# A pair of experts' scatter in the middle of the next odd expert, in float32r with bare one-hots

## The chip, the cores and the metric

One Trainium2 chip, one of its cores. The metric is device time in microseconds (us) of one execution. The engines are named as in the profile: PE is TensorE's matmul (PEld its weight load), DVE is VectorE, ACT is ScalarE, POOL is GpSimd, SP is SyncE, which issues the DMAs.

## The reference, cut to what matters

256 tokens of width 1024 pass a mixing layer (an SSD group beside an MLA group), and then a mixture of experts, in which each token goes to 4 of 32 experts:

```python
def moe_ffn(h, w_router, b_router, w_gate_up, b_gate_up, w_down, b_down):
    logits = (h @ w_router).astype(jnp.float32) + b_router.astype(jnp.float32)
    top_vals, top_idx = lax.top_k(logits, TOP_K)
    gates = jax.nn.softmax(top_vals, axis=-1)
    ...
    def expert_block(args):
        tok, g, e = args
        xb = h[tok]
        gu = xb @ w_gate_up[e] + b_gate_up[e]
        glu = jnp.minimum(gu[:, :D_FF_EXPERT], SWIGLU_LIMIT)
        lin = jnp.clip(gu[:, D_FF_EXPERT:], -SWIGLU_LIMIT, SWIGLU_LIMIT)
        act = glu * jax.nn.sigmoid(SWIGLU_ALPHA * glu) * (lin + 1.0)
        y = act @ w_down[e] + b_down[e]
        return y * g[:, None].astype(y.dtype)
    ...
    return jax.ops.segment_sum(y.reshape(n_slots, d), slot_tok, num_segments=n_tok)
```

All weights are float32: 8 MB of w_gate_up and 4 MB of w_down for each expert, 384 MB in all.

## The kernel before, in words

The mixing layer and the router take the first 185 us. Then a loop runs over the experts e = 0 to 31 (`last` is 31). For each expert there are four weight tiles of 2 MB for the way up (gu{e}_0 to gu{e}_3) and two for the way down (dn{e}_0, dn{e}_1). They come through one DMA queue of SP, in a fixed order (L230), into nine slots of 2 MB; a transfer starts when the matmuls that read its slot's last content have ended. Four experts (0, 2, 3, 31) give their first tile free early ("ahead"); the others give all four up tiles free at the end of the way up.

An expert has room for 64 tokens (CAP). Its tokens are gathered by a matmul with one-hot columns (`gather`, oh on DVE, pg on PE L1231, copied to xg), transposed (`gathered`, pgt L1239) and modulated on DVE in two steps (xT, L1241 and L1242). `up` (L1252) multiplies by the weights, tile for tile; `act` copies the sums (gs), transposes them (tp, L1272), adds the bias on DVE (u), and makes the minimum, the sigmoid (ACT) and two products (sg, ac; L1284 to L1288). `down` (L1300) multiplies ac by the down tiles into one PSUM buffer (py), and `keep_down` copies it into half of each of two tiles (cm0, cm1), so that two experts, an even one and the odd one before or after it, fill them together. `scatter` (L1332 to L1339) adds such a pair's rows to the tokens' sums: four sums of 128x512 (pc, two PSUM buffers), each one matmul of the gated one-hots (gtm) by cm, added to acc by DVE. In f32 one such matmul shows as two instructions in the trace. The gated one-hots are made by `spread_cols` (go, eight instructions on DVE) and `spread_mats` (four transposes L1324, an ACT copy L1326). PSUM: one buffer (tag "sm") serves pg and both pgt, one serves py, tp and pc have two.

PE's order is the program's; DVE's and ACT's is made by a scheduler. In iteration e PE does: the first up tile; gather of e+1; down of e-1 (`finish_down`); the second up tile; the transposes of xT for e+1; the other two up tiles; the transposes of act(e). For even e the scatter of the pair (e-2, e-1) stands between the way up and act(e) (for e = 30 it is the pair (28,29), behind act(30)), and four transposes for the pair's one-hots follow act. Tokens beyond 64 of an expert are handled in a branch (`overflow`), which stands behind up, for the four experts "ahead" behind the first up tile; whether it is taken is known only on the chip, and all engines read the count at that place (releaser names with a q, as DVEq L1417, are waits for an engine to come to such a branch). In the loop's last two iterations the order differs: down(29) is ahead of up(30), down(30) ahead of up(31), and the last pair (30, 31) is scattered after the loop.

The lines of before that matter most:

```python
        gs = up_out(gu, "g1b", A.copy if e == last else V.tensor_copy)
        if not ahead:
            overflow(e, wg, wd, f"pr{(e + ahead) % 2}")
        ...
        pair = e > 0 and e % 2 == 0
        if pair and e < last - 1:
            scatter(lambda t, ch: gt[:, ch, t, :], lambda ch: comb[ch], bias)
        ...
        ac = act(e, gs, 2 if e == last else 1)
        if pair and e == last - 1:
            scatter(lambda t, ch: gt[:, ch, t, :], lambda ch: comb[ch])
```

## Time and profile before

| | |
|---|---|
| median of 3 runs | 1159.1 us (1157.83 to 1161.47) |
| the profiled execution's own time | 1159.5 us |
| its span | 1157.7 us, granted clock 0.977 on the mean |
| PE busy | 1069.6 us (92%) |
| DVE, ACT, POOL busy | 419.8, 191.1, 69.5 us |
| DMA | 449.21 MB, 388 GB/s on the mean |

The span is from the first instruction to the last; the time has 1.8 us more around it. Busy shares are means over stages with different limits, so they don't tell which engine a microsecond on the path belongs to. The granted clock is TensorE's, as a share of full speed. A row of the timeline gives start, duration, engine, line, what is written from what, how many instructions are merged, and in brackets the idle time of that engine before them with what ended it.

### The profile page before, as it was taken

The page shows a single profiled execution, that of the slowest core. Times are in us where ns is not written, and L with a number is a line of the kernel's source. Part 1 is how long each engine was busy: PE and PEld are TensorE (multiplying, and loading weights), DVE is VectorE, ACT ScalarE, POOL GpSimd, SP SyncE. Part 2 cuts the span into 40 slices and gives each one's busy share as a digit, 9 for nine tenths or more (in the row PEclk, how much of TensorE's full clock was granted, in tenths as well). Part 3 has the DMA queues.
Part 4 walks back from the last instruction along what each step waited for, and adds up shares of the span by engine and source line. Part 5 has one row for each costly group of instructions (what it writes and reads, how often), then busy time and mean ns, then how long its engine had stood idle before and what let it go on. Part 6 is the DMA issues. An engine that isn't in the chain of part 4 may idle for free. (4 is left out here: it accounts for less than half of the span.)

```text
span 1157.7 us, 13070 instructions
## 1 busy us (share of the span) xinstructions
PE 1069.6 (92%) x5125; PEld 456.0 (39%) x5128; DVE 419.8 (36%) x892; ACT 191.1 (17%) x366; POOL 69.5 (6%) x68
## 2 busy tenths in 40 slices
PE   5999998989999999899989998999899998999996
PEld 3886674333333333333323332333323332333333
DVE  3358755333333323232322333142313232323224
ACT  5464433110111111001000101010101010101003
POOL 0274330000000000000000000000000000000000
PEclk9999999999999999899989999999989998999998
DMA  9959679968989999999999999999999999999982
GB/s 341 354 227 368 243 280 417 380 266 354 412 351 427 427 427 429 426 428 427 427 427 428 428 427 427 428 428 425 430 427 428 426 429 428 420 421 428 428 357 74
DMA packets 47713, 449.21 MB, mean 388 GB/s; under 512 B 6741, under 2 KB 11062, under 8 KB 21210
## 3 DMA queue, kind: packets, MB, share of 16 engines
q1 hardware_dynamic: 47162, 447.41, 93.0%
q8 instruction: 75, 1.23, 0.4%
q14 instruction: 60, 0.49, 0.1%
q10 hardware_dynamic: 416, 0.07, 0.0%
HBM read 446.42 MB, written 1.05 MB: 387 GB/s over the span
## 5 line engine op out<-in xcount | busy, mean ns | idle before, releaser
L1252 PE MATMUL gu<-gu,xT 128*64 128x512 f32 x2048 | 474.8, 612 | 30.5 <-DMA gu<-in_w_gate_up 28.5
L1252 PEld LDWEIGHTS gu<-gu,xT 128*64 128x64 f32 x2048 | 146.5, 140 | 308.9 <-issue 272.4
L1300 PE MATMUL py<-dn,ac 128*64 128x512 f32 x992 | 218.9, 594 | 0.2 <-DVE ac L1288 0.2
L1300 PEld LDWEIGHTS py<-dn,ac 128*64 128x64 f32 x992 | 70.7, 137 | 143.0 <-issue 133.6
L1309 DVE COPY cm<-py 64x512 f32<-64x512 f32 x30 | 20.8, 694 | 210.9 <-ACT cm L1308 210.9
L1258 DVE COPY gs<-gu 128x512 f32<-128x512 f32 x31 | 21.4, 692 | 174.9 <-PE gu L1252 174.9
L1257 ACT COPY gs<-gu 128x512 f32<-128x512 f32 x32 | 18.8, 586 | 317.5 <-PE gu L1252 317.5
L1338 PE MATMUL pc<-cm,gtm 128*128 128x512 f32 x120 | 59.3, 620 | 11.7 <-DVEq L1417 10.3
L1231 PE MATMUL pg<-x,oh 128*64 128x512 f32 x256 | 60.6, 594 | 3.6 <-DVEq L1417 1.9
L1339 DVE TENSOR_TENSOR acc<-acc,pc 128x512 f32<-128x512 f32 x64 | 44.0, 688 | 38.2 <-PE pc L1338 38.1
L1596 POOL TENSOR_TENSOR x<-x,acc 128x512 f32<-128x512 f32 x1 | 1.3, 1263 | 917.8 <-ACT acc L1595 917.8
L1241 DVE TENSOR_TENSOR xT<-pgt,md 128x512 f32<-128x512 f32 x32 | 22.1, 692 | 86.4 <-PE pgt L1239 86.4
L1279 DVE TENSOR_TENSOR u<-tp,biasT 128x512 f32<-128x512 f32 x64 | 41.5, 685 | 29.5 <-PE tp L1272 29.3
L1308 ACT COPY cm<-py 64x512 f32<-64x512 f32 x30 | 17.4, 579 | 189.6 <-PE py L1300 189.6
L1272 PEld LDWEIGHTS tp<-ident,gs 128*128 128x128 f32 x256 | 34.8, 208 | 27.8 <-ACTq L1417 16.4
L1227 DVE TENSOR_SCALAR oh<-cst,rkp,r 128x64 f32<-128x64 f32 x64 | 17.2, 311 | 76.8 <-PE pg L1231 76.8
L1272 PE MATMUL tp<-ident,gs 128*128 128x128 f32 x256 | 38.2, 290 | 6.5 <-PEq L1417 5.3
L1338 PEld LDWEIGHTS pc<-cm,gtm 128*128 128x128 f32 x120 | 19.3, 188 | 51.3 <-DVEq L1417 20.0
L1233 ACT COPY xg<-pg 128x512 f32<-128x512 f32 x32 | 18.7, 586 | 121.8 <-PE pg L1231 121.7
L1285 ACT ACTIVATE sg<-u 128x512 f32<-128x512 f32 (+1 forms) x33 | 20.4, 618 | 95.3 <-DVE u L1284 91.8
L1231 PEld LDWEIGHTS pg<-x,oh 128*64 128x64 f32 x256 | 18.1, 137 | 40.9 <-issue 39.9
L1316 DVE TENSOR_SCALAR go<-cst,rkp,gate 128x64 f32<-128x64 f32 x128 | 30.0, 308 | 0.6 <-DVEq L1417 0.6
(432 smaller groups left out, 943.3 us busy)
## 6 DMA issues: line engine op xcount, KB each, us to landing
gu<-in_w_gate_up SPq DMA_DIRECT2D x128, 2048.0 KB, 21.4
dn<-in_w_down SPq DMA_DIRECT2D x62, 2048.0 KB, 29.1
w2w<-in_w_ada SPq DMA_DIRECT2D x6, 1024.0 KB
w0w<-in_w_ada SPq DMA_DIRECT2D x5, 1024.0 KB, 6.9
w0w<-in_w_ada SPq DMA_DIRECT2D x6, 512.0 KB, 6.5
w2w<-in_w_ada SPq DMA_DIRECT2D x6, 512.0 KB
w4w<-in_w_ada SPq DMA_DIRECT2D x3, 1024.0 KB, 8.7
w4w<-in_w_out SPq DMA_DIRECT2D x3, 1024.0 KB
```

Source lines behind the costliest of these rows:

```text
L1231: T.matmul(pg[64 * h : 64 * h + 64, :], oh[:, t, :], x[:, t, h * 512 : h * 512 + 512], start=t == 0, stop=t == TT - 1)
L1241: V.tensor_tensor(xT.rearrange("p (h q) s -> p q h s", h=2), pg, a2.rearrange("p (h q) -> p q h", h=2)[:, :, :, None].to_broadcast([P, 4, ...
L1252: T.matmul(gu[h][64 * g : 64 * g + 64, :], xT[:, k, :], ws(k)[:, g * 1024 + h * 512 : g * 1024 + h * 512 + 512], start=k == 0, stop=k == K ...
L1258: copy(gs[1], gu[1])
L1272: T.transpose(tp[f // 4][:, f % 4].rearrange("p g s -> p (g s)"), gs[f // 4][:, rows_of(f % 4)], ident)
L1279: V.tensor_tensor(u[:, hs], tp[h], bv[:, hs, :, None].to_broadcast([P, 4, 2, CAP]), op=OP.add)
L1285: A.activation(sg[:, fs], u[:, fs, 0, :], AF.Sigmoid, scale=1.702)
L1300: T.matmul(py[64 * g : 64 * g + 64, :], ac[:, f, :], wd(f, ch), start=f == 0, stop=f == FT - 1)
L1309: V.tensor_copy(comb[(e & 1) ^ 1][64:128, :], py[64:128, :])
L1316: V.tensor_scalar(go[:, t, j, :], iota, rkp[:, t, ee : ee + 1], gate[:, t, ee : ee + 1], op0=OP.is_equal, op1=OP.mult)
L1338: T.matmul(pc, lhs(t, ch), rhs(ch), start=bias is None or (t, ch) != bias_left[0], stop=True)
L1339: V.tensor_tensor(acc[:, t, ch * 512 : ch * 512 + 512], acc[:, t, ch * 512 : ch * 512 + 512], pc, op=OP.add)
```

## The change

The scatter of a pair moves. In an even expert it no longer stands between up and act; the pair (e-2, e-1) is scattered in the next iteration, e+1, behind down(e) and ahead of the second up tile. For e = 30 the pair (28, 29) is scattered between the second and the third up tile. The operands change: the one-hots are bare (is_gt on DVE, from PSUM, in place of the ACT copy), the gate of each row is the sum of its gated one-hots (a reduction on DVE), and `gated` (in place of the copies) multiplies the down result by it into two float32r tiles, hi and lo, of which ACT makes hi and DVE lo; each sum of a scatter has then two float32r matmuls. The overflow's scatter changes in the same way. The last pair stays in f32 with gated one-hots. The one-hots for a gather (`slots`) are formed an expert earlier.

```diff
@@ -1220,11 +1220,14 @@
     acc = tl([P, TT, D], "acc", "f1")
     iota = cst[:, CIO : CIO + CAP]
-    def gather(e):
-
+    def slots(e):
         oh = tl([P, TT, CAP], "oh", f"oh{e % 2}")
         for t in range(TT):
             V.tensor_scalar(oh[:, t, :], iota, rkp[:, t, e : e + 1], r2[:, t : t + 1], op0=OP.is_equal, op1=OP.mult)
+        return oh
+
+    def gather(oh):
+
         pg = mp.tile([P, 512], F32, tag="sm", name="pg")
         for t in range(TT):
             for h in range(2):
@@ -1301,12 +1304,18 @@
                          start=f == 0, stop=f == FT - 1)
         return py
+    def gated(hi, lo, src, by):
+
+        A.activation(hi, src, AF.Copy, scale=by)
+        V.scalar_tensor_tensor(lo, src, by, hi, op0=OP.mult, op1=OP.subtract)
+
     def keep_down(e, py):
         if e % 2 == 0:
-            comb[0] = tl([P, 512], "cm0", "pv2")
-            comb[1] = tl([P, 512], "cm1", "bn")
-        A.copy(comb[e & 1][0:64, :], py[0:64, :])
-        V.tensor_copy(comb[(e & 1) ^ 1][64:128, :], py[64:128, :])
+            for ch in range(2):
+                comb[ch] = [tl([P, 512], f"c{j}{ch}", (("pv2", "cl0"), ("bn", "cl1"))[ch][j], F32R) for j in range(2)]
+        for g in range(2):
+            ch, r = (e & 1) ^ g, slice(64 * g, 64 * g + 64)
+            gated(comb[ch][0][r, :], comb[ch][1][r, :], py[r, :], gts[-1][1][r, ch : ch + 1])
     def spread_cols(es):
@@ -1316,15 +1325,23 @@
                 V.tensor_scalar(go[:, t, j, :], iota, rkp[:, t, ee : ee + 1], gate[:, t, ee : ee + 1], op0=OP.is_equal, op1=OP.mult)
         return go
-    def spread_mats(go, tag="bgr"):
+    turn = [0]
+
+    def spread_mats(go, bare=True):
         pg = mp.tile([P, 2, TT, P], F32, tag="sm", name="pgt")
         for ch in range(2):
             for t in range(TT):
                 T.transpose(pg[:, ch, t, :], go[:, t, 2 * ch : 2 * ch + 2, :].rearrange("p j s -> p (j s)"), ident)
-        gt = tl([P, 2, TT, P], "gtm", tag)
-        A.copy(gt, pg)
-        return gt
+        gt = tl([P, 2, TT, P], "gtm", ("bgr", "bgr1")[turn[0]] if bare else "cbs", F32R if bare else F32)
+        if not bare:
+            A.copy(gt, pg)
+            return gt
+        V.tensor_scalar(gt, pg, 0.0, None, op0=OP.is_gt)
+        by = tl([P, 2], f"by{turn[0]}")
+        turn[0] = 1 - turn[0]
+        V.tensor_reduce(by, pg.rearrange("p c t q -> p c (t q)"), axis=AX.X, op=OP.add)
+        return gt, by
     bias_left = [(t, ch) for t in range(TT) for ch in range(2)]
@@ -1335,7 +1352,9 @@
                 pc = mp.tile([P, 512], F32, tag=tag, name="pc", bufs=2)
                 if bias is not None and (t, ch) == bias_left[0]:
                     T.matmul(pc, bias[:, t, :], end[0:NE, D + ch * 512 : D + ch * 512 + 512], start=True, stop=False)
-                T.matmul(pc, lhs(t, ch), rhs(ch), start=bias is None or (t, ch) != bias_left[0], stop=True)
+                hi, lo = rhs(ch)
+                T.matmul(pc, lhs(t, ch), hi, start=bias is None or (t, ch) != bias_left[0], stop=False)
+                T.matmul(pc, lhs(t, ch), lo, start=False, stop=True)
                 V.tensor_tensor(acc[:, t, ch * 512 : ch * 512 + 512], acc[:, t, ch * 512 : ch * 512 + 512], pc, op=OP.add)
     def warm(n):
@@ -1376,7 +1396,8 @@
         for t in range(TT):
             for ch in range(2):
                 T.transpose(pg[:, t, ch, :], go[:, t, ch : ch + 4].rearrange("p j s -> p (j s)"), ident)
-        A.copy(ovt, pg)
+        V.tensor_scalar(ovt, pg, 0.0, None, op0=OP.is_gt)
+        V.tensor_reduce(by, pg.rearrange("p t c q -> p (t c q)"), axis=AX.X, op=OP.add)
         gu = mp.tile([P, 512], F32, tag="py", name="guo")
         for k in range(KT):
             for j in range(4):
@@ -1397,9 +1418,10 @@
         V.tensor_scalar(u[:, :, 1], u[:, :, 1], -7.0, 1.0, op0=OP.max, op1=OP.add)
         V.tensor_tensor(ovs, ovs, u[:, :, 0], op=OP.mult)
         V.tensor_tensor(ovs, ovs, u[:, :, 1], op=OP.mult)
-        return ovt
-
-    def ov_down(wd, ovt):
+        return ovt, by
+
+    def ov_down(wd, spread):
+        ovt, by = spread
         py = mp.tile([P, 512], F32, tag="py", name="pyo")
         for i in range(4):
             for z in range(2):
@@ -1407,8 +1429,8 @@
                 for ch in range(2):
                     o = 64 * z + 32 * ch
                     T.matmul(py[o : o + OV, :], ovs[:, f % 4, f // 4, :], wd(f, ch), start=i == 0, stop=i == 3)
-        yo = tl([P, 512], "yo", "md1")
-        A.copy(yo, py)
+        yo = [tl([P, 512], f"yo{j}", ("md1", "pt1")[j], F32R) for j in range(2)]
+        gated(*yo, py, by)
         scatter(lambda t, ch: ovt[:, t, ch, :], lambda ch: yo)
     def overflow(e, wg, wd, tag):
@@ -1450,8 +1472,10 @@
         return end[:, 0:D]
     G.memset(acc, 0.0)
-    gs = wd = gt = None
-    xT = gathered(0, gather(0))
+    gs = wd = gt = bias = None
+    gts = []
+    xT = gathered(0, gather(slots(0)))
+    oh = slots(1)
     e4 = tl([P, TT, 4], "e4")
     tc.keep_in_program_order(V.tensor_tensor(e4, m8[:, :, 0:4], m8[:, :, 0:1].to_broadcast([P, TT, 4]), op=OP.subtract))
     A.activation(e4, e4, AF.Exp)
@@ -1473,11 +1497,21 @@
         return lambda k: ts_[k // 2][:, k % 2 * 2 * FF : k % 2 * 2 * FF + 2 * FF]
     def finish_down(e, ac, wd):
-        keep_down(e, down(e, ac, wd, e & 1))
+
+        py = down(e, ac, wd, e & 1)
+        if e % 2 == 0 and e > 0:
+            scatter_pair(gts[-2])
+        keep_down(e, py)
         for j in range(2):
             st_.done(f"dn{e}_{j}")
-    bias = None
+    def scatter_pair(gt):
+        nonlocal bias
+        scatter(lambda t, ch: gt[0][:, ch, t, :], lambda ch: comb[ch], bias)
+        if bias is not None:
+            bias_left.pop(0)
+            bias = bias if bias_left else None
+
     last = ne - 1
     for e in range(ne):
         wg = weights_up(e)
@@ -1496,7 +1530,9 @@
             overflow(e, wg, wd, f"pr{(e + ahead) % 2}")
             st_.done(f"gu{e}_0")
         if e < last - 1:
-            xg = gather(e + 1)
+            xg = gather(oh)
+            if e < last - 2:
+                oh = slots(e + 2)
         if 0 < e < last - 1:
             finish_down(e - 1, ac, wdp)
         up(gu, xT, wg, range(2, 4))
@@ -1506,6 +1542,8 @@
             go = spread_cols((e, e + 1, e + 1, e))
         if e == 19:
             g2b = gain()
+        if e == last - 1:
+            scatter_pair(gts[-1])
         up(gu, xT, wg, range(4, 8))
         xT = xTn if e < last - 1 else xTl
         gs = up_out(gu, "g1b", A.copy if e == last else V.tensor_copy)
@@ -1516,23 +1554,15 @@
         if e == 9:
             end = late[0]
             bias = gates_by_expert()
-        pair = e > 0 and e % 2 == 0
-        if pair and e < last - 1:
-            scatter(lambda t, ch: gt[:, ch, t, :], lambda ch: comb[ch], bias)
-            if bias is not None:
-                bias_left.pop(0)
-                bias = bias if bias_left else None
         ac = act(e, gs, 2 if e == last else 1)
-        if pair and e == last - 1:
-            scatter(lambda t, ch: gt[:, ch, t, :], lambda ch: comb[ch])
-        if e == last - 1:
+        if e % 2 == 0 and e < last - 1:
+            gts.append(spread_mats(go))
+        elif e == last - 1:
             gt = gtl
-        elif e % 2 == 0:
-            gt = spread_mats(go)
         if e == last - 2:
-            xTl = gathered(last, gather(last))
-            gtl = spread_mats(spread_cols((last - 1, last - 1, last, last)), "cbs")
+            xTl = gathered(last, gather(slots(last)))
+            gtl = spread_mats(spread_cols((last - 1, last - 1, last, last)), False)
     tc.keep_in_program_order(A.activation(epsw, epsc, AF.Sqrt))
```

How the instructions stand at three places. The first is the end of expert 2 and the middle of expert 3. On PE from the end of up(2) to the first up tile of expert 3, before (gu_2 and gu_3 are expert 2's last two up tiles, pc<-cm the scatter of the pair (0,1)):

```order
L1252 MATMUL gu<-gu_2_2061,xT 64x512 x8
L1252 MATMUL gu<-gu_3_2429,xT 64x512 x8
L1338 MATMUL pc<-cm_2055,gtm 128x512
L1338 MATMUL pc<-cm_2056,gtm 128x512
L1338 MATMUL pc<-cm_2055,gtm 128x512
L1338 MATMUL pc<-cm_2056,gtm 128x512
L1272 MATMUL tp<-ident,gs_2733 128x128 x4
L1272 MATMUL tp<-ident,gs_2734 128x128 x4
L1324 MATMUL pgt<-ident,go 128x128 x4
L1252 MATMUL gu<-gu_0_2435,xT 64x512 x8
```

In the change:

```order
L1255 MATMUL gu<-gu_2_2078,xT 64x512 x8
L1255 MATMUL gu<-gu_3_2462,xT 64x512 x8
L1275 MATMUL tp<-ident,gs_2776 128x128 x4
L1275 MATMUL tp<-ident,gs_2777 128x128 x4
L1335 MATMUL pgt<-ident,go 128x128 x4
L1255 MATMUL gu<-gu_0_2468,xT 64x512 x8
```

The scatter's four matmuls are gone from here. They stand in expert 3 now, on PE between down(2) (py) and the second up tile (gu_1), with c as the gated down results in their two parts:

```order
L1234 MATMUL pg<-x,oh 64x512 x4
L1303 MATMUL py<-dn_0_2464,ac 64x512 x8
L1303 MATMUL py<-dn_1_2466,ac 64x512 x8
L1356 MATMUL pc<-c_2068,gtm 128x512
L1357 MATMUL pc<-c_2069,gtm 128x512
L1356 MATMUL pc<-c_2070,gtm 128x512
L1357 MATMUL pc<-c_2071,gtm 128x512
L1356 MATMUL pc<-c_2068,gtm 128x512
L1357 MATMUL pc<-c_2069,gtm 128x512
L1356 MATMUL pc<-c_2070,gtm 128x512
L1357 MATMUL pc<-c_2071,gtm 128x512
L1255 MATMUL gu<-gu_1_2698,xT 64x512 x8
```

Each of the four sums is two matmuls now, one for hi and one for lo, and the second up tile stands behind them. On DVE the same place, act(2), before (gs the copied sums, acc<-acc,pc the scatter's additions; the last two rows read the count for the overflow's branch):

```order
L1258 COPY gs_2734<-gu 128x512
L1339 TENSOR_TENSOR acc<-acc,pc 128x512 x4
L1279 TENSOR_TENSOR u<-tp,biasT 128x512 x2
L1316 TENSOR_SCALAR go<-cst,rkp,gate 128x64 x8
L1284 TENSOR_SCALAR u<-u 128x1024
L1286 TENSOR_SCALAR u<-u 128x8x64
L1287 TENSOR_TENSOR sg<-sg,u 128x512
L1288 TENSOR_TENSOR ac<-sg,u 128x512
L1416 TENSOR_LOAD cnt
L1417 COMPARE_AND_BRANCH
```

In the change:

```order
L1261 COPY gs_2777<-gu 128x512
L1282 TENSOR_TENSOR u<-tp,biasT 128x512 x2
L1340 TENSOR_SCALAR gtm<-pgt 128x512
L1343 TENSOR_REDUCE by_2813<-pgt 128x2
L1325 TENSOR_SCALAR go<-cst,rkp,gate 128x64 x3
L1287 TENSOR_SCALAR u<-u 128x1024
L1325 TENSOR_SCALAR go<-cst,rkp,gate 128x64 x5
L1289 TENSOR_SCALAR u<-u 128x8x64
L1290 TENSOR_TENSOR sg<-sg,u 128x512
L1291 TENSOR_TENSOR ac<-sg,u 128x512
L1438 TENSOR_LOAD cnt
```

The four additions are gone from here; is_gt (gtm) and the reduction (by) stand between u and the minimum, and five of the one-hots stand behind the minimum.

The second place is the start of the loop on DVE, before (xT are the two steps of expert 0's gathered rows; e, d, eq and gate are the softmax over the four chosen experts; the eight gated one-hots of the pair (0,1), go, follow behind the branch):

```order
L1227 TENSOR_SCALAR oh<-cst,rkp,r_1523 128x64 x4
L1241 TENSOR_TENSOR xT<-pgt,md_112 128x4x2x64
L1242 TENSOR_TENSOR xT<-xT,md_112 128x512
L1456 TENSOR_TENSOR e_1717<-m_1525 128x8
L1459 TENSOR_REDUCE d_1720<-e_1717 128x2
L1460 RECIPROCAL d_1720<-d_1720 128x2
L1461 TENSOR_TENSOR e_1717<-e_1717,d_1720 128x8
L1463 TENSOR_TENSOR eq<-eq,e_1717 128x128 x2
L1464 TENSOR_REDUCE gate<-eq 128x64
L1416 TENSOR_LOAD cnt
L1417 COMPARE_AND_BRANCH
```

In the change:

```order
L1226 TENSOR_SCALAR oh<-cst,rkp,r_1523 128x64 x2
L1480 TENSOR_TENSOR e_1720<-m_1525 128x8
L1483 TENSOR_REDUCE d_1723<-e_1720 128x2
L1484 RECIPROCAL d_1723<-d_1723 128x2
L1485 TENSOR_TENSOR e_1720<-e_1720,d_1723 128x8
L1226 TENSOR_SCALAR oh<-cst,rkp,r_1523 128x64 x2
L1487 TENSOR_TENSOR eq<-eq,e_1720 128x128 x2
L1488 TENSOR_REDUCE gate<-eq 128x64
L1244 TENSOR_TENSOR xT<-pgt,md_112 128x4x2x64
L1325 TENSOR_SCALAR go<-cst,rkp,gate 128x64 x5
L1245 TENSOR_TENSOR xT<-xT,md_112 128x512
L1325 TENSOR_SCALAR go<-cst,rkp,gate 128x64 x3
```

The softmax stands ahead of xT's first step now, and five of the eight one-hots stand between xT's two steps.

The third place is the end of expert 30 on PE, before (tp are act(30)'s transposes, pc the scatter of the pair (28,29), py is down(30), gu_0 expert 31's first up tile):

```order
L1272 MATMUL tp<-ident,gs_13277 128x128 x4
L1272 MATMUL tp<-ident,gs_13278 128x128 x4
L1338 MATMUL pc<-cm_12783,gtm 128x512
L1338 MATMUL pc<-cm_12784,gtm 128x512
L1338 MATMUL pc<-cm_12783,gtm 128x512
L1338 MATMUL pc<-cm_12784,gtm 128x512
L1300 MATMUL py<-dn_0_13159,ac 64x512 x8
L1300 MATMUL py<-dn_1_13161,ac 64x512 x8
L1252 MATMUL gu<-gu_0_13163,xT 64x512 x8
```

In the change:

```order
L1275 MATMUL tp<-ident,gs_13829 128x128 x4
L1275 MATMUL tp<-ident,gs_13830 128x128 x4
L1303 MATMUL py<-dn_0_13693,ac 64x512 x8
L1303 MATMUL py<-dn_1_13695,ac 64x512 x8
L1255 MATMUL gu<-gu_0_13697,xT 64x512 x8
```

Down(30) follows the transposes directly; the scatter of the pair stands within up(30).

## Rows read from the trace of the kernel before

**Rows 1.** The page's slices: PE's busy tenths, the DMA engines' share, GB/s.

```profile
PE   5999998989999999899989998999899998999996
...
DMA  9959679968989999999999999999999999999982
GB/s 341 354 227 368 243 280 417 380 266 354 412 351 427 427 427 429 426 428 427 427 427 428 428 427 427 428 428 425 430 427 428 426 429 428 420 421 428 428 357 74
```

**Rows 2.** The page's DMA issues: count, KB each, median us to landing.

```profile
gu<-in_w_gate_up SPq DMA_DIRECT2D x128, 2048.0 KB, 21.4
```

**Rows 3.** Timeline of PE, experts 6 to 9: start us, us, instructions, [idle before].

```profile
395.58 3.89 PE L1338 MATMUL pc<-cm,gtm 128*128 128x512 f32 x8 [1.03 <-DVEq L1417]
399.31 1.11 PE L1272 MATMUL tp<-ident,gs 128*128 128x128 f32 x8
...
400.79 3.65 PE L1252 MATMUL gu<-gu,xT 128*64 128x512 f32 x16
...
424.63 1.21 PE L1272 MATMUL tp<-ident,gs 128*128 128x128 f32 x8 [0.40 <-PEq L1417]
...
455.19 3.23 PE L1252 MATMUL gu<-gu,xT 128*64 128x512 f32 x14
```

**Rows 4.** The waits of PE by releaser: us in total, times, longest.

```profile
PE gu L1252 <- DMA gu<-in_w_gate_up: 28.5, 12, 5.3
```

**Rows 5.** Timeline of PE at weight waits of experts 10, 14 and 28.

```profile
483.07 5.39 PE L1252 MATMUL gu<-gu,xT 128*64 128x512 f32 x12 [1.98 <-DMA gu<-in_w_gate_up]
...
602.76 6.41 PE L1252 MATMUL gu<-gu,xT 128*64 128x512 f32 x16 [4.59 <-DMA gu<-in_w_gate_up]
...
1020.42 5.35 PE L1252 MATMUL gu<-gu,xT 128*64 128x512 f32 x16 [1.94 <-DMA gu<-in_w_gate_up]
```

**Rows 6.** Windows: busy us of each engine, granted clock, DMA share, GB/s.

```profile
335.00:340.00 5.00, 5.00 (x26) 1.71 (x24) 0.17 (x1) 0.04 (x1) 0.00 (x0) 1.00 0.55 231
340.00:345.00 5.00, 4.71 (x15) 1.73 (x12) 2.82 (x5) 0.55 (x1) 0.00 (x0) 1.00 0.66 208
...
600.00:612.00 12.00, 9.24 (x30) 2.84 (x32) 2.19 (x5) 1.14 (x2) 0.00 (x0) 0.72 1.01 429
```

**Rows 7.** Timeline of SP's queue: the issue that up(4) holds back.

```profile
340.86 0.33 SPq L230 DMA_DIRECT2D gu<-in_w_gate_up  x1
```

**Rows 8.** Timeline of PE, two float32r matmuls of L482 to L484.

```profile
170.22 0.39 PE L482 MATMUL pm<-whi,mix 128*128 128x512 f32 x1
170.45 0.39 PE L483 MATMUL pm<-whl,mix 128*128 128x512 f32 x1
```

**Rows 9.** Groups of DVE instructions: count | busy us, mean ns | idle before.

```profile
L1339 DVE TENSOR_TENSOR acc<-acc,pc 128x512 f32<-128x512 f32 x64 | 44.0, 688 | 38.2 <-PE pc L1338 38.1
...
L817 DVE TENSOR_REDUCE mx<-at 128x2 f32<-128x512 f32 x4 | 2.7, 687 | 0.4 <-PE at L815 0.4
```

**Rows 10.** Timeline of PE and of DVE, expert 0.

```profile
190.04 3.65 PE L1252 MATMUL gu<-gu,xT 128*64 128x512 f32 x16 [1.51 <-DVE xT L1242]
...
215.50 1.08 PE L1300 MATMUL py<-dn,ac 128*64 128x512 f32 x4 [0.21 <-DVE ac L1288]
...
192.45 1.88 DVE L1316 TENSOR_SCALAR go<-cst,rkp,gate 128x64 f32<-128x64 f32 x8 [0.56 <-DVEq L1417]
```

**Rows 11.** Timeline of PE, from the scatter behind up(2) to gather(4).

```profile
285.12 3.96 PE L1338 MATMUL pc<-cm,gtm 128*128 128x512 f32 x8
288.91 1.12 PE L1272 MATMUL tp<-ident,gs 128*128 128x128 f32 x8
...
295.97 1.94 PE L1231 MATMUL pg<-x,oh 128*64 128x512 f32 x8 [1.91 <-DVEq L1417]
```

**Rows 12.** Timeline of PE, experts 29 to 31: up(29), act(30), down(30).

```profile
1051.54 3.65 PE L1252 MATMUL gu<-gu,xT 128*64 128x512 f32 x16
...
1102.88 1.20 PE L1272 MATMUL tp<-ident,gs 128*128 128x128 f32 x8 [0.40 <-PEq L1417]
...
1109.09 7.09 PE L1300 MATMUL py<-dn,ac 128*64 128x512 f32 x32
```

More of the change, by code (lines that the diff above doesn't have):

```diff
@@ L1349, in ov_up @@
     def ov_up(e, rk, wg, tag):
-        ovt = tl([P, TT, 2, P], "ovt", tag)
+        ovt = tl([P, TT, 2, P], "ovt", tag, F32R)
+        by = tl([P, 1], "ovb")
         io = iota[:, :OV]
```

## The prediction

> **What bounds the kernel now.** I read the slices first [rows 1]: from the thirteenth of 40 on (about 345 us) the transfers run at 420 to 430 GB/s until the last two, while TensorE (PE) is also busy at 0.9. A weight tile has 2048 KB [rows 2], so at 428 GB/s one arrives every 2.097 MB / 428 GB/s = 4.90 us, an expert (six tiles) every 29.4 us and a pair every 58.8. PE needs less: from the first up matmul of expert 7 to that of expert 9 it takes 455.19 - 400.79 = 54.4 us without a wait for a weight [rows 3]. So PE catches up, and from 483.07 on it waits for weights, 12 times, 28.5 us in all, the last time at 1020.42 [rows 4, 5]. The reader is to see three stretches. (1) Up to 345 us slots come free late: in 335 to 345 the transfers run at 0.55 and 0.66 of their share, and the next tile is issued at 340.86, behind the end of up(4) on PE [rows 6, 7]. Whatever delays PE before that moves the whole stream. (2) From 345 to about 1050 the stream is the clock, and PE work is free there. (3) After 1050 PE waits for no weight any more, and each us on PE is a us at the end [rows 4, 5, 12].
>
> The change takes work out of stretch 2, where it is free, and puts work into stretches 1 and 3.
>
> **One scatter.** Now: 8 listed f32 matmuls, 3.7 us from their start to that of the next work [rows 3]. After: 8 float32r matmuls, two for each of four sums. Nearest row: 128x512 matmuls of the three-product projection follow each other every 0.23 us at the full clock [rows 8], so PE alone needs 8 x 0.23 = 1.84. Each sum is then added on DVE in 0.69 [rows 9], and there are two PSUM buffers: the third sum waits for the first addition (0.46 + 0.1 + 0.69 = 1.25), the fourth for the second (1.94 and the release), and PE is through at about 2.65. Bounds 1.84 and 3.9; I take 2.65, since the additions are the same instructions as now.
>
> **The start (stretch 1).** (a) In the order of the change five of the eight gate one-hots stand on DVE between the two steps of expert 0's xT, for which up(0) waits. Eight take 1.88 [rows 10], so five take 1.2, and up(0)'s wait grows from 1.51 to 2.7: +1.2. (b) In act(0) is_gt and the reduction stand ahead of the minimum. Neither shows in the trace; 128x512 out of PSUM takes 0.69 in the additions and in a reduction [rows 9], so 1.38, of which the five one-hots that now go behind the minimum give back 0.45: ac(0) is 0.9 later, and down(0) waits for it already now, 0.21 [rows 10]. Behind down(0) all of PE's work is queued: +0.9 (bounds 0 and 1.4). (c) The scatter of pair (0,1) leaves the place between up(2) and its transposes. These start at 288.91, after the scatter's start at 285.12; without it they start 0.4 after the end of up(2) (that is what expert 7 shows), 3.4 earlier. But gather(4) does not wait for PE: it stands behind a branch that DVE reaches after act(2), 1.91 us later than PE [rows 11]. That chain on DVE gains 1.38 (is_gt, reduction) and loses some 0.3, as five one-hots now fill the wait for the sigmoid: 1.1 net. So gather(4) comes 3.4 - 1.1 = 2.3 earlier, and its wait grows from 1.91 to about 3.0: -2.3. (d) The scatter itself now stands after down(2), ahead of up(3): +2.65. (e) The overflow of expert 1 and the scatter of pair (2,3) change place by a few tenths with both signs; I take 0 (bounds -1.2 and +0.7). Sum: 1.2 + 0.9 - 2.3 + 2.65 = +2.45 at 340.86, and with it on the stream.
>
> **The middle.** An even expert loses 3.7 and the wait ahead of it (1.03) and gets 0.4 back ahead of the transposes; its down waits about 1.1 for ac; the odd expert gains 2.65: 54.4 - 4.3 + 1.1 + 2.65 = 53.9 a pair, below 58.8. Gating while copying makes two instructions of one for each half (one on ACT, one on DVE, the latter like the additions 0.7); the PSUM buffer is next wanted an expert later, about 25 us. One-hots formed an expert earlier lie where DVE is idle. All this costs nothing while the stream binds; it would cost its full price if PE had to bind there. SP's queue gets no new transfer.
>
> **The end (stretch 3).** gu29_0 is the first tile for which PE does not wait: it is used at 1051.54 [rows 12]; by six tiles after 1020.42 it was there at about 1049.8, at the earliest. I take 1050.6 (no row shows the landing; bounds 0 and 1.7 us of slack). In the change PE comes to that tile about 4 us earlier and starts when it lands: -0.9. After that there are two scatters that PE cannot hide: pair (26,27) after down(28), +2.65, and pair (28,29) within up(30), +2.65. In exchange the old scatter between the transposes of act(30) and down(30) goes: the distance of 1109.09 - 1102.88 = 6.2 [rows 12] shrinks to what act takes without one-hots and additions on DVE: from the transposes of act(2) to the branch behind it are 295.97 - 288.91 = 7.06, and 1.88 of that are eight one-hots [rows 10, 11], so 5.1. That is -1.1. PE then stands idle for 5.1 - 1.2 = 3.9 us, where it now scatters. Sum: +3.3.
>
> **The clock.** After a long wait PE runs at half its clock for a while: expert 14's first 16 matmuls, after 4.59 us, take 6.41 instead of 3.65, and those of expert 28, after 1.94, take 5.35; after 1.91 and 1.51 nothing happens [rows 3, 5, 10, 11]. [...] So such a wait costs 1.7 to 2.8 us; I take 2.8, as the waits here are nearer the long ones. The change puts PE into four such waits on the path: up(0) after 2.7, gather(4) after 3.0, up(29) after some 4, down(30) after 3.9. [...] By the rows alone the waits before up(0) and gather(4) lie between the 1.98 and the 4.59 of [rows 5], and the one at up(29) depends on how PE and the stream stand there, so I count three of the four: 3 x 2.8 = +8.4.
>
> **Sum.** 2.45 + 3.3 + 8.4 = +14.2 us. Against the profiled execution's own 1159.5 (1157.7 span and 1.8 around it) this gives 1173.7; that execution is 0.4 above the median of 1159.1, so I predict **1173.3** for the median.
>
> **Rivals.**
> - *All four waits cost the clock*: + 2.8, 1176.1. For it: the three waits of 1.94 and more that are shown all did so. Chance 0.25. Three as forecast: 0.30 (1170.5 to 1175).
> - *One or two do*: 1167.7 to 1170.5; the wait before up(29) shrinks if PE comes late out of expert 27, and 1.91 and 1.51 went without. Chance 0.17.
> - *None does*: + 5.8, 1164.9. Chance 0.08.
> - *The stream hides it, no change*: scatters at 1.84 (the additions overlap better than I think) take 0.8 off each of three, 2.4; go and the act chain are off the path (-2.1, as the scheduler's order on DVE may meet a late gather anyway): 5.8 - 4.5 = +1.3, 1160.4, if no clock is lost. Against it: down(0) waits for DVE now. Chance 0.13, for all that lies within 0.3% (3.5 us, about what a measurement of this kernel can tell from no change).
> - *Faster*: DVE ahead of gather(4) decides. If its new instructions lie beside other waits, so that it reaches that branch when PE does, the full 3.4 and the old wait of 1.91 are saved, 5.3 instead of 2.3, (a) and (b) fall away by the same, and the float32r scatter costs 1.84: -5.3 + 1.84 = -3.5 at 340.86, which the 4 us of starved transfers between 335 and 345 (0.45 and 0.34 of 5 us each) allow. If a last tile then ends the kernel and not PE, it reaches the end: 1155.6. It turns on a chain of DVE that is 3 us shorter than its instructions add up to; against it speak the 1.91 and that PE waits for no weight at the end. Chance 0.07.
>
> **How the numbers follow.** 1173.3 is the likeliest case. Slower by over 0.3%: 0.25 + 0.30 + 0.17 + 0.08 = 0.80; same 0.13; faster 0.07. The range goes from 1162.0, where the case without lost clock and with half its other terms ends, to 1178.0, all four waits and a scatter some 0.7 dearer; it leaves out the faster case and most of "no change". The likeliest side's own range is 1164.9 to 1178.
>
> **What the profile of the changed kernel would show.** Scatter matmuls after down(2) within 2.4 to 2.9 us, DVE additions between them; up(0) after a wait of 2.7 on xT; gather(4) after 3 us on DVE's branch; the issue of gu5_3 at 343 to 349 instead of 340.86; about 4 us of wait before the first up tile of nearly every odd expert, then the clock at half; after 1053 no wait for a weight, down(30) behind a wait of 3.9 for ac, and the first matmuls of up(29) and down(30) at twice their time. It is wrong if the waits do not lower the clock, if the scatter takes 1.8, if a weight is waited for after up(29), or if gather(4) comes as soon as PE is free.

## The result and the profile after

The changed kernel takes 1171.88 us (median of 4 runs, 1168.79 to 1172.93) against 1159.51 for the kernel before (4 runs, 1157.83 to 1161.47): a ratio of 1.0106, 95% interval 1.0089 to 1.0122. It is slower by 12.4 us; the forecast was 14.2 us slower, 1173.3 in a range of 1162 to 1178. The profiled execution has a span of 1169.7, 12.0 more than before.

First some of PE's waits in the changed kernel (us in total, times, longest), beside [rows 4]:

```profile
PE gu L1255 <- DMA gu<-in_w_gate_up: 49.0, 18, 5.8
...
PE pc L1356 <- DVE acc L1358: 4.8, 15, 0.4
PE py L1303 <- DVEq L1439: 4.1, 1, 4.1
...
PE gu L1255 <- DVE xT L1245: 2.5, 1, 2.5
PE pg L1234 <- DVEq L1439: 2.2, 1, 2.2
```

PE waits longer for weights than before (49.0 against 28.5 us). That is the middle, and not where the 12 us are lost: PE has less to do there, and waits instead. The wait for xT is 2.5 where it was 1.51 [rows 10]; new is one of 4.1 ahead of a down. PE's timeline at the start of the loop, beside [rows 10, 11] (up(0), down(0), gather(4), the first, fifth and last rows around the scatter of pair (0,1), then the second up tile of expert 3):

```profile
189.52 5.35 PE L1255 MATMUL gu<-gu,xT 128*64 128x512 f32 x16 [2.50 <-DVE xT L1245]
...
216.57 7.09 PE L1303 MATMUL py<-dn,ac 128*64 128x512 f32 x32 [0.96 <-DVE ac L1291]
...
293.98 1.94 PE L1234 MATMUL pg<-x,oh 128*64 128x512 f32 x8 [2.15 <-DVEq L1439]
...
302.72 0.50 PE L1356 MATMUL pc<-c,gtm 128*128 128x512 f32 x1
...
304.29 0.50 PE L1356 MATMUL pc<-c,gtm 128*128 128x512 f32 x1 [0.37 <-DVE acc L1358]
...
305.55 3.65 PE L1255 MATMUL gu<-gu,xT 128*64 128x512 f32 x16
```

Up(0) waits 2.50, and its 16 matmuls take 5.35 where they took 3.65 (granted clock 0.68 on the mean from 189.50 to 194.90). Gather(4) comes at 293.98 instead of 295.97, and waits 2.15 without a loss of clock (1.00 from 293.98 to 295.90). The scatter takes 305.55 - 302.72 = 2.83, with a wait for an addition in its middle. The transfer that up(4) holds back, beside [rows 7]:

```profile
341.86 0.33 SPq L230 DMA_DIRECT2D gu<-in_w_gate_up  x1
```

It is issued 1.0 later than before. That makes the change look better than it is, for the loop's first gather stands earlier in this execution. Here it is in the changed kernel and, in the second line, in the kernel before:

```profile
183.60 1.94 PE L1234 MATMUL pg<-x,oh 128*64 128x512 f32 x8 [0.27 <-DVE cnt L1216]
185.12 1.94 PE L1231 MATMUL pg<-x,oh 128*64 128x512 f32 x8 [0.27 <-DVE cnt L1216]
```

The instructions ahead of it are the same, and its place varies by execution (before_again, below). Counted from there the issue is 2.5 later. The windows around it, and one in the middle where the share drops a little (columns as in [rows 6]):

```profile
335.00:340.00 5.00, 5.00 (x26) 1.72 (x24) 1.13 (x2) 0.00 (x0) 0.00 (x0) 1.00 0.75 320
340.00:345.00 5.00, 4.60 (x28) 2.21 (x24) 2.74 (x5) 0.59 (x1) 0.00 (x0) 1.00 0.45 116
880.00:910.00 30.00, 29.23 (x136) 10.72 (x134) 10.38 (x17) 3.17 (x5) 0.00 (x0) 1.00 0.98 411
```

At the end of the loop (up(29); the scatter of (26,27) and the tile behind it; down(29); the scatter of (28,29) and the tile behind it; act(30)'s transposes; down(30)), beside [rows 12]:

```profile
1053.93 5.46 PE L1255 MATMUL gu<-gu,xT 128*64 128x512 f32 x16 [5.82 <-DMA gu<-in_w_gate_up]
...
1067.91 0.50 PE L1356 MATMUL pc<-c,gtm 128*128 128x512 f32 x1
...
1070.68 3.65 PE L1255 MATMUL gu<-gu,xT 128*64 128x512 f32 x16
...
1089.02 8.42 PE L1303 MATMUL py<-dn,ac 128*64 128x512 f32 x32
...
1104.24 0.50 PE L1356 MATMUL pc<-c,gtm 128*128 128x512 f32 x1
...
1107.02 7.09 PE L1255 MATMUL gu<-gu,xT 128*64 128x512 f32 x32
1114.50 1.21 PE L1275 MATMUL tp<-ident,gs 128*128 128x128 f32 x8 [0.40 <-PEq L1439]
1119.79 8.40 PE L1303 MATMUL py<-dn,ac 128*64 128x512 f32 x32 [4.08 <-DVEq L1439]
```

From up(29)'s start to the end of the span it takes 1169.7 - 1053.9 = 115.8 us, before 1157.7 - 1051.5 = 106.2. So 9.6 us are lost here. Counted from the loop's first gather the whole loss is 13.5 us: 2.5 at gu5_3's issue, 1.4 more at up(29), and these 9.6; the earlier start takes 1.5 off, which leaves 12.0. Two scatters stand on the path (2.8 each), down(30) starts 5.3 after the transposes and not 6.2, and three bursts are slow: up(29) with 5.46 instead of 3.65, down(29) 8.42 and down(30) 8.40 instead of 7.09.

### The profile page after: what moved, and what is told of

Its sections match the earlier page's. It is cut to its first block, busy times and chain, and to the rows that moved or that the text cites. A ratio compares the mean times of both kernels' runs of the same rounds, so it can differ in the third digit from the quotient of the medians.

```text
span 1169.7 us, 13181 instructions
## 1 busy us (share of the span) xinstructions
PE 1054.1 (90%) x5125; PEld 454.1 (39%) x5128; DVE 459.0 (39%) x955; ACT 205.3 (18%) x380; POOL 67.5 (6%) x68
## 3 DMA queue, kind: packets, MB, share of 16 engines
HBM read 446.42 MB, written 1.05 MB: 383 GB/s over the span
## 5 line engine op out<-in xcount | busy, mean ns | idle before, releaser
L1303 PEld LDWEIGHTS py<-dn,ac 128*64 128x64 f32 x992 | 73.3, 138 | 148.2 <-issue 146.3
L1310 DVE SCALAR_TENSOR_TENSOR c<-py,by,c 64x512 fp32r<-64x512 f32 x60 | 44.9, 748 | 130.9 <-ACT c L1309 130.9
L1309 ACT ACTIVATE c<-py,by 64x512 fp32r<-64x512 f32 x60 | 41.0, 683 | 249.8 <-PE pc L1356 120.3
L1356 PE MATMUL pc<-c,gtm 128*128 128x512 f32 x60 | 28.3, 472 | 4.5 <-DVE acc L1358 4.5
L1242 PEld LDWEIGHTS pgt<-ident,xg 128*128 128x128 f32 x128 | 17.7, 207 | 27.9 <-issue 24.3
```

The source lines that it names most:

```text
L1303: T.matmul(py[64 * g : 64 * g + 64, :], ac[:, f, :], wd(f, ch), start=f == 0, stop=f == FT - 1)
L1309: A.activation(hi, src, AF.Copy, scale=by)
L1310: V.scalar_tensor_tensor(lo, src, by, hi, op0=OP.mult, op1=OP.subtract)
L1356: T.matmul(pc, lhs(t, ch), hi, start=bias is None or (t, ch) != bias_left[0], stop=False)
```

## The experiments

"Before" in a row is the kernel before, run on the same chip between them. It was 1158.0 to 1159.5, so times from different chips are best compared by their distance to it; the changed kernel stood 12.4 above it at first and 14.4 in after_again.

| run | median us | before | ratio, 95% interval |
|---|---|---|---|
| tail_one | 1168.13 | 1158.67 | 1.0084 (1.0061 to 1.0106) |
| tail_two | 1165.40 | 1158.67 | 1.0062 (1.0045 to 1.0078) |
| not_moved | 1167.59 | 1158.67 | 1.0076 (1.0060 to 1.0093) |
| move_alone | 1167.38 | 1158.67 | 1.0069 (1.0050 to 1.0088) |
| operands_alone | 1164.35 | 1157.97 | 1.0056 (1.0038 to 1.0074) |
| slots_late | 1171.66 | 1157.97 | 1.0116 (1.0096 to 1.0137) |
| middle_only | 1162.59 | 1157.97 | 1.0039 (1.0021 to 1.0057) |
| warm_two | 1167.88 | 1157.97 | 1.0089 (1.0069 to 1.0108) |
| after_again | 1173.92 | 1159.48 | 1.0119 (1.0097 to 1.0140) |
| deferred_e4 | 1158.84 | 1159.48 | 0.9996 (0.9984 to 1.0009) |
| deferred_e14 | 1155.68 | 1159.48 | 0.9969 (0.9954 to 0.9984) |

The first theory was that the place costs: scatters leave the stretch that the stream hides and go where PE sets the end. The rival was that the operands cost (float32r halves, bare one-hots, gates applied while copying).

**tail_one**: the last scatter of the loop back behind act(30).

```diff
-        if e == last - 1:
-            scatter_pair(gts[-1])
         up(gu, xT, wg, range(4, 8))
...
         ac = act(e, gs, 2 if e == last else 1)
+        if e == last - 1:
+            scatter_pair(gts[-1])
```

> The changed kernel, with only the scatter of pair (28,29) back behind act(30), still in float32r with bare one-hots. Theory (the place costs: work out of the stretch that the stream hides, into the end): the 2.8 us within up(30) go, and the scatter fills PE's wait of 4.1 us before down(30), so that down(30) keeps its clock (7.1 instead of 8.4); its additions may put 0.9 into act's chain: 3.2 to 4.2 us below the changed kernel, about 1168. Rival (the operands cost: two products for each copy, is_gt and the reduction on DVE, two matmuls for one): no change beyond 0.5 us.

1168.13, and on the path from up(29) to the end 112.7 instead of 115.8: down(30) takes 7.09 again. As expected of the place (3.75 below the changed kernel; 2.9 by the distance to the kernel before).

**tail_two**: the pair (26,27) goes back too.

```diff
-        if e % 2 == 0 and e > 0:
+        if e % 2 == 0 and e > 0 and e not in (28,):
             scatter_pair(gts[-2])
...
+        if e in (28,):
+            scatter_pair(gts[-1])
         ac = act(e, gs, 2 if e == last else 1)
...
```

> As tail_one, and the scatter of pair (26,27) also back between up(28) and act(28). Theory: it lies in PE's wait for gu29_0 (5.8 us in the changed kernel) again and costs nothing there, so another 2.8 us go, about 1165; if the shorter wait of some 3 us still lowers the clock, nothing more, otherwise 1.8 more. Rival (operands): the same time as the changed kernel.

1165.40: another 2.7, the price of one scatter. Up(29) now waits 2.55 and is slow all the same (5.35). So the two pairs at the end make about 6.5 of the 12 us (5.6 by the distance to the kernel before).

**not_moved**: the same for all pairs, so that every scatter stands in its old place.

> The changed kernel with every scatter in its old place: float32r, bare one-hots and gating while copying stay, only the move is undone. Theory (place): nearly all comes back, 1160 to 1162; what stays is up(0)'s later start (1.2 and 1.7 us for the clock) less what a scatter in float32r saves at expert 2 (1.1). Rival (operands): 1169 to 1172, as the changed kernel.

1167.59: the theory of the place alone is refuted. With every scatter where it was, 8.9 us of loss remain, though the rival said more (1169 to 1172). And it is 2.2 slower than tail_two (the intervals overlap): with these operands, moving the pairs from (0,1) to (24,25) cost nothing and may have gained. In its profile gather(4) waits 2.91 and takes 3.26, and gu5_3's issue stands 4.1 later than before, counted from the first gather, against 2.4 in tail_two.

**move_alone**: the other half; f32, gated one-hots through ACT's copy and plain copies of the down results, in the new places.

```diff
-        keep_down(e, down(e, ac, wd, e & 1))
+        py = down(e, ac, wd, e & 1)
+        if e % 2 == 0 and e > 0:
+            scatter_pair(gts[-2])
+        keep_down(e, py)
...
-            gt = spread_mats(go)
+            gts.append(spread_mats(go, ("bgr", "bgr1")[e // 2 % 2]))
```

> The kernel before with the move alone: scatters in f32 with gated one-hots (ACT copy, two buffers for them), in the places of the change. Theory (place): as slow as the change or slower, since an f32 scatter takes 3.8 instead of 2.8 twice at the end, and without the delay of up(0): 1169 to 1174. Rival (operands): 1158 to 1161.

1167.38, below what was expected of the place, and far above the rival's. Its timeline of PE (gather(4); the scatter of (26,27) and the tile behind it; act(30)'s transposes; down(30)):

```profile
290.18 1.94 PE L1231 MATMUL pg<-x,oh 128*64 128x512 f32 x8 [1.15 <-DVEq L1417]
...
1063.08 3.89 PE L1338 MATMUL pc<-cm,gtm 128*128 128x512 f32 x8
1066.90 3.65 PE L1252 MATMUL gu<-gu,xT 128*64 128x512 f32 x16
...
1110.19 1.20 PE L1272 MATMUL tp<-ident,gs 128*128 128x128 f32 x8 [0.47 <-PEq L1417]
1115.48 9.77 PE L1300 MATMUL py<-dn,ac 128*64 128x512 f32 x32 [4.09 <-DVEq L1417]
```

An f32 scatter costs 1066.90 - 1063.08 = 3.8 on the path, and down(30), after 4.09, takes 9.77. From up(29) to the end it is 117.5. But gather(4) waits only 1.15 there: without is_gt and the reduction DVE's chain is shorter, and counted from the loop's first gather (183.0) gu5_3's issue is only 0.4 later than before. So the move alone costs nearly nothing at the start and 11.3 at the end. Move and operands each cost almost 9 us alone (8.7; 8.9 in not_moved), and together 12. Of what they share the rows show two terms: a scatter 1 us cheaper, twice, at the end, and 1.6 less at the start than in not_moved; the rest is not shown.

**operands_alone**: as not_moved, and the one-hots of a gather are formed where they were. The lines by which the two differ:

```diff
     xT = gathered(0, gather(slots(0)))
-    oh = slots(1)
...
-            xg = gather(oh)
-            if e < last - 2:
-                oh = slots(e + 2)
+            xg = gather(slots(e + 1))
```

> Every scatter in its old place and the gather's one-hots formed where they were (so the start of the loop is that of the kernel before); float32r, bare one-hots and gating while copying stay. Theory (the operands cost only by what they do to the start, up(0)'s longer wait and its clock): 1157 to 1161. Rival (the operands cost everywhere, by DVE's and ACT's longer chains ahead of gather, down and the PSUM buffers): 1164 to 1168, as not_moved.

1164.35: at the lower edge of the rival's 1164 to 1168, and above the theory's 1157 to 1161. On PE's timeline gather(4), up(29), act(30)'s transposes and down(30):

```profile
294.73 1.94 PE L1234 MATMUL pg<-x,oh 128*64 128x512 f32 x8 [2.91 <-DVEq L1439]
...
1052.65 3.65 PE L1255 MATMUL gu<-gu,xT 128*64 128x512 f32 x16 [2.57 <-DMA gu<-in_w_gate_up]
...
1103.92 1.20 PE L1275 MATMUL tp<-ident,gs 128*128 128x128 f32 x8 [0.40 <-PEq L1439]
...
1110.35 9.64 PE L1303 MATMUL py<-dn,ac 128*64 128x512 f32 x32 [1.06 <-DVE ac L1291]
```

Gather(4) waits 2.91 where it waited 1.91. In the changed kernel, which has the same operands, is_gt and the reduction start 0.6 apart on DVE (288.45 and 289.05), and its chain in act(2) from the first addition of the bias to the end of ac takes 6.73 (287.05 to 293.78) instead of 5.85. Act(30) to down(30) is 6.43 instead of 6.21, and down(30) is slow (9.64) after a wait of 1.06. From up(29) to the end it is 108.9 against 106.2, nearly all of it that one burst. It is slow although the old scatter stands ahead of it again.

**slots_late**: the last diff alone, on the changed kernel, with every scatter in its new place.

> The changed kernel with the gather's one-hots formed where they were, so that the eight gate one-hots stand behind xT at the start again. Theory: up(0) waits 1.5 and keeps its clock, the stream is 1 to 2.9 us earlier, 1168.5 to 1171. Rival (the start is hidden in later waits): 1171 to 1173.

1171.66, what the rival said: up(0) waits 1.51 and takes 3.65 again, yet the time hardly moves (1.0116 against 1.0106). Gather(4) and down(30) in that execution:

```profile
290.95 3.63 PE L1234 MATMUL pg<-x,oh 128*64 128x512 f32 x8 [2.15 <-DVEq L1439]
...
1117.95 10.02 PE L1303 MATMUL py<-dn,ac 128*64 128x512 f32 x32 [4.09 <-DVEq L1439]
```

Gather(4), after the same 2.15 as in the changed kernel, took 3.63 instead of 1.94, and down(30) 10.02 instead of 8.40. Counted from the first gather (182.5) gu5_3's issue is 2.3 later than before, against 2.5. What the start gained, the slower bursts took in this execution.

**middle_only**: new places only for the pairs (2,3) to (24,25), otherwise operands_alone. The line that tells them apart, against the changed kernel:

```diff
-        if e % 2 == 0 and e > 0:
+        if e % 2 == 0 and e > 0 and e not in (2, 28):
             scatter_pair(gts[-2])
...
```

> The scatters of pairs (2,3) to (24,25) in the new places, those of (0,1), (26,27) and (28,29) in their old ones, gather's one-hots as before, float32r operands. Theory (the new place is free where the stream binds): the same as operands_alone within 1.5 us. Rival (the move costs in the middle too, through waits that lower the clock and slots that come free late): 2 to 4 us above operands_alone.

1162.59, 1.8 below operands_alone where at most 1.5 was expected, and just inside its interval: twelve moved pairs cost nothing. With tail_two, and with the 0.4 of move_alone at gu5_3's issue, this places the move's price at the end.

**warm_two**: the changed kernel with matmuls that nobody reads in two waits.

```diff
         ac = act(e, gs, 2 if e == last else 1)
+        if e == last - 1:
+            warm(15)
...
             gts.append(spread_mats(go))
+            if e == last - 3:
+                warm(20)
```

> The changed kernel with matmuls that no one reads in two of PE's waits: 20 before up(29), 15 between act(30)'s transposes and down(30). Nothing is taken away. Theory (waits lower the clock): up(29)'s first 16 matmuls 3.65 instead of 5.46, down(30) 7.1 instead of 8.4, the time 3.1 us below the changed kernel, 1168.8. Rival (what is slow there is not the clock but the operands' arrival): no change, or slower by up to 1.

1167.88, 4.0 below the changed kernel, with more work on PE; its distance to the kernel before is 9.9, where the changed kernel had 12.4 and 14.4. Its timeline (gather(4); the 20 matmuls and up(29); down(29); the 15 matmuls and down(30)):

```profile
292.97 3.14 PE L1234 MATMUL pg<-x,oh 128*64 128x512 f32 x8 [2.15 <-DVEq L1439]
...
1050.23 4.48 PE L1363 MATMUL warm<-scr,onesb 128*128 128x512 bf16 x20
1054.65 3.65 PE L1255 MATMUL gu<-gu,xT 128*64 128x512 f32 x16
...
1087.62 7.09 PE L1303 MATMUL py<-dn,ac 128*64 128x512 f32 x32
...
1113.34 3.40 PE L1363 MATMUL warm<-scr,onesb 128*128 128x512 bf16 x15 [0.36 <-DVE u L1282]
1116.90 7.09 PE L1303 MATMUL py<-dn,ac 128*64 128x512 f32 x32 [0.17 <-issue]
```

Up(29) is back to 3.65, down(30) to 7.09; down(29) also, which had no matmuls ahead of it. The windows of up(29)'s burst in the changed kernel and, in the second line, here (columns as in [rows 6]), show the granted clock at 0.64 on the mean and at 1.00:

```profile
1054.00:1059.00 5.00, 5.00 (x16) 1.60 (x18) 0.00 (x0) 0.00 (x0) 0.00 (x0) 0.64 1.01 433
1054.70:1058.30 3.60, 3.60 (x19) 1.29 (x20) 1.37 (x2) 0.00 (x0) 0.00 (x0) 1.00 1.00 428
```

The 0.64 is made up of 0.50 from 1054 to 1057, 0.69 in the microsecond behind it and 1.00 from 1058 on. Down(29) and down(30) of the changed kernel show the same: 0.50 in 1089.00 to 1091.00 and in 1119.80 to 1122.00, and 0.84 over each burst. From up(29) to the end it is 110.9 in warm_two. So the slow bursts are the clock, and cost 4.9 of the end's 9.6. The first row shows the opposite at the start: gather(4), after 2.15, takes 3.14 here, and the first tile of expert 2 takes 5.16 instead of 3.65. Gu5_3's issue stands 5.6 later than before, counted from the first gather (181.2), against 2.5 in the changed kernel, with the same instructions up to there.

**after_again**: the changed kernel, unedited.

> The changed kernel once more. Theory (after a wait the clock falls in some executions and not in others, and the mixing layer's end is not at the same place each time): the same 1170 to 1173, but other bursts than in the first profile (up(0), gather(4), up(29), down(29), down(30)) at half the clock, and gather(0) 0.5 to 1.5 us away from its first place. Rival (the length of the wait decides): the same bursts slow as before, within 0.3 us.

1173.92, with the same bursts slow: up(0) 5.35, up(29) 5.23, down(29) 8.22, down(30) 9.99, and gather(4) after 2.15 not (1.94). That is 0.9 above the range expected, and the first gather is only 0.3 from its first place. The pattern repeated, as the rival said; but down(30) differs by 1.6 (9.99 against 8.40), more than the rival's 0.3, and in warm_two, the same program up to its first added matmuls, other bursts were slow. Two executions don't make it a rule.

**deferred_e4 and deferred_e14**: if the start costs 1 to 1, work should leave it. The kernel before, f32, with pair (0,1) kept until expert 4; or every pair two experts longer until 14. The diff is that of deferred_e14, with 4 for 14 in the other:

```diff
-            comb[0] = tl([P, 512], "cm0", "pv2")
-            comb[1] = tl([P, 512], "cm1", "bn")
+            comb[0] = tl([P, 512], "cm0", ("pv2", "cl0")[e // 2 % 2])
+            comb[1] = tl([P, 512], "cm1", ("bn", "cl1")[e // 2 % 2])
...
-            scatter(lambda t, ch: gt[:, ch, t, :], lambda ch: comb[ch], bias)
...
+            late_pairs.append((gt, list(comb)))
+            while len(late_pairs) > (1 if e < 14 else 0):
+                gp, cp = late_pairs.pop(0)
+                scatter(lambda t, ch: gp[:, ch, t, :], lambda ch: cp[ch], bias)
...
-            gt = spread_mats(go)
+            gt = spread_mats(go, ("bgr", "bgr1")[e // 2 % 2])
```

> The kernel before, in f32, with one pair moved: (0,1) is not scattered at expert 2 but at expert 4, with (2,3), behind up(4) and so behind the last transfer that a slot held back; two more copies of the down results and a second buffer of one-hots. Theory (work leaves the start and goes where the stream hides it): gather(4) some 4 us earlier, gu5_3's issue at 337, the stream 3 to 4 us earlier to its end: 1154.5 to 1156.5 against 1158 to 1159. Rival (the start is not what the stream hangs on, or PE then comes late to the slots behind): 1157.5 to 1161.

> As deferred_e4, but each pair waits two experts longer until expert 14, which scatters two pairs; so at no place before 600 us two scatters follow each other. Theory: 1154.5 to 1156.5, as deferred_e4, or 0.5 better if two scatters at expert 4 delay slots there. Rival: as there, 1157.5 to 1161.

deferred_e4 gains nothing (0.9996), deferred_e14 3.8 us (1155.68, 0.9969; by the interval 1.9 to 5.3): faster than both kernels. Windows of deferred_e4, columns as in [rows 6]:

```profile
350.00:360.00 10.00, 10.00 (x50) 3.25 (x48) 2.35 (x5) 1.17 (x2) 0.00 (x0) 1.00 1.00 424
360.00:370.00 10.00, 9.60 (x47) 3.26 (x42) 1.91 (x3) 0.58 (x1) 0.00 (x0) 1.00 0.79 336
370.00:380.00 10.00, 10.00 (x50) 3.91 (x51) 4.49 (x9) 1.22 (x2) 0.00 (x0) 1.00 0.96 372
380.00:390.00 10.00, 10.00 (x50) 3.62 (x48) 2.08 (x3) 0.58 (x1) 0.00 (x0) 1.00 1.02 436
```

In deferred_e4 gu5_3's issue is 4.1 earlier than before, counted from the first gather. But behind the double scatter at expert 4 (7.83 us from 336.84) the transfers starve once more (0.79 and 0.96 of their share in 360 to 380), and up(29) stands only 0.3 earlier. In deferred_e14 they don't starve:

```profile
360.00:370.00 10.00, 9.60 (x50) 3.76 (x48) 4.48 (x7) 1.22 (x2) 0.00 (x0) 1.00 1.01 426
370.00:380.00 10.00, 10.00 (x50) 3.31 (x46) 1.23 (x3) 1.16 (x2) 0.00 (x0) 1.00 1.00 428
```

Its first gather, its gather(4), its one scatter at expert 4 and its up(29):

```profile
182.55 1.94 PE L1231 MATMUL pg<-x,oh 128*64 128x512 f32 x8 [0.27 <-DVE cnt L1216]
...
290.21 1.94 PE L1231 MATMUL pg<-x,oh 128*64 128x512 f32 x8 [1.16 <-DVEq L1417]
...
335.26 3.95 PE L1338 MATMUL pc<-cm,gtm 128*128 128x512 f32 x8 [0.29 <-PEq L1417]
...
1047.36 3.65 PE L1252 MATMUL gu<-gu,xT 128*64 128x512 f32 x16
```

Gather(4) stands 107.7 after the loop's first gather, before 110.9 after it: 3.2 earlier. But up(29) on PE is only 1.6 earlier by the same count (864.8 against 866.4), without a wait, and the end behind it as long as before. So in this profile about half of the 3.2 reaches the end; the rest of its shorter span comes from the earlier first gather, which varies by execution.

**before_again**: the kernel before, unedited, one execution.

> The kernel before, unedited, once more. Theory (the place of the loop's first gather varies between executions of one kernel): it stands 1 us or more away from the 185.1 us of the first profile, and the rest of the loop moves with it. Rival (it hangs on the kernel): within 0.3 us of 185.1.

Its first gather stands at 183.10, 2.0 earlier than in the first profile; gu5_3's issue at 338.91, 2.0 earlier; up(29) at 1049.92, 1.6 earlier; the span is 1156.1, 1.6 shorter:

```profile
183.10 1.94 PE L1231 MATMUL pg<-x,oh 128*64 128x512 f32 x8 [0.27 <-DVE cnt L1216]
...
1049.92 3.65 PE L1252 MATMUL gu<-gu,xT 128*64 128x512 f32 x16
```

So the place of the loop's start varies by execution, and in this pair, without any edit, 1.6 of the 2.0 us gained there reached the end.

## Why the prediction was right, and where not

**What bounds.** Three stretches, and the middle free: shown by middle_only (twelve pairs, free within the intervals) against tail_two (2.7 us for a pair). One bound was wrong: the first stretch does not end at 345. deferred_e4 shows that PE's work at 341 still costs transfers at 360 to 380. No term of the sum rested on that. PE's waits for weights came 18 times, but not with about 4 us ahead of nearly every odd expert: 4.8 at experts 13, 19 and 23, 1.8 to 2.4 at 15, 17, 25 and 27, and expert 21 kept its clock after 3.60 (granted 1.00 from 813.87 to 817.52). In the changed kernel the stream also lost about 1 us between 790 and 930 (424 GB/s on the mean against 427 before; 0.98 of its share at 880 to 910). That was not forecast, and its cause stays open.

**One scatter**, 2.65: measured 2.83, 2.77 and 2.78. PE waits for an addition in its middle (0.37 <-DVE acc), as said.

**The start**, +2.45: measured +2.5, counted from the loop's first gather, with about 0.9 of the clock in it. (The issue itself stands at 341.86, below the 343 to 349 named, because the loop began 1.5 earlier.) (a) up(0)'s wait 2.50 for 2.7. (b) down(0) waits 0.96 for 1.1, though the 0.45 that the sum gives back there stands on no row (by (a) five one-hots take 1.2). Up(0)'s slow burst adds 1.7, but about half of that is gone by act(0): down(0) stands 2.6 later (216.57 - 183.6 = 33.0 against 215.50 - 185.1 = 30.4). (c) Gather(4) comes 3.1 earlier than that, not 2.3 (293.98 - 183.6 = 110.4 against 295.97 - 185.1 = 110.9). From the transposes to gather(4) it is 7.79 instead of 7.06, so DVE's chain grew by 0.7 and not by the 1.1 that I added up, and PE waits 2.15 there for 3.0. (d) 2.83. So the sum is right by errors that cancel, and that is luck.

**The end**, +3.3 without the clock: two scatters 2.8 each, act(30) -0.9 for -1.1. PE waits for the landing of gu29_0, as said; whether that gave back the 0.9 no row shows. From up(29) on, 9.6 = 5.6 - 0.9 + 4.9 for the clock.

**The clock**, +8.4 for three of four bursts at 2.8 each: the step whose size was off. Measured were four bursts, 1.7 (up(0)), 1.8, 1.3 and 1.3, together 6.1, and not the four that I named: gather(4) kept its clock after 2.15, and down(29) lost it behind three shorter waits (0.40, 1.05 and 0.84 in the trace). The rows of before gave a price of 1.7 to 2.8; two of the four lie at its lower end and two below it. In other executions down(30) alone cost 2.7 to 2.9 (9.77, 10.02 and 9.99 in move_alone, slots_late and after_again, for 7.09), so the size is one execution's. At the end of the loop up(29) after 5.82 takes 5.46, and behind warm_two's matmuls 3.65. At a shorter wait it goes both ways: gather(4) after 2.15 takes 1.94 in the changed kernel and 3.63 in slots_late.

**What I did not see.** In the sum the operands' price stood only in (b) and in 1.1 of (c), and in the middle they were put at nothing. operands_alone shows 6.4 us, without (a). Its trace, counted from the first gather (183.4), shows 0.5 at gu5_3's issue, 2.3 more at up(29), and 2.7 from there to the end, 2.6 of it down(30)'s burst. Why the operands cost the 2.3 stays open. So the forecast came as near as it did partly by luck. Without the clock the sum gave 5.8, and the profile, counted from the first gather, has 7.7 (13.5 less 0.9 and 4.9); the clock was put at 8.4 and cost 5.8. That the operands' price and the move's overlap (8.7 and 8.9 alone, 12.4 together) was not forecast either.

## What to carry to other kernels

Ask of each moved piece in which stretch it was and in which it will be: a piece that the stream hides was free (middle_only), and the same piece cost about 3 us where PE sets the end (2.7 in tail_two) or the first slots (3.2 at gather(4), saved by deferred_e14); so what can wait should leave the start and go to the middle, one at a time (deferred_e14). An empty place on PE was not free either: the burst behind it ran slow in places (up(29) after 5.82: 5.46 for 3.65, at a granted clock of 0.50 from 1054 to 1057), and work that filled it (the old scatter behind act(30), in tail_one) gave 3.1 us from up(29) to the end: its own 2.8 and 1.3 of the clock, less 1.1 that ac came later. It is no guarantee: in operands_alone and not_moved the scatter stood there, and down(30) took 9.64 and 8.78 after waits of 1.06 and 1.27. An operand trick that saves 1 us on PE (2.8 for 3.8 a scatter) is to be charged with what it adds to the chain on DVE that PE waits for (6.73 for 5.85 in act(2)).
